# A two-layer decoder trunk: the seven-product form of the first FFN product begins at column tile 2 instead of 4

## The chip, the cores and the metric

The kernel runs on one core of one Trainium2 chip. The metric is the device time of one execution in microseconds, as the median of several executions.

## The reference

Two consecutive layers work on 512 tokens of width 1024 in float32. Each layer is a mixer and then a SwiGLU feed-forward network (FFN). The change is in the FFN, which runs once in each layer:

```
h = modulate(rms_norm(x, ffn_norm[layer]), sh2, sc2)      # (512, 1024)
gate, up = split(h @ w1, 2)                               # w1 (1024, 2 * 2816)
x = x + g2 * ((silu(gate) * up) @ w2)                     # w2 (2816, 1024)
```

## The kernel before

**Precision.** Every large product is made of three matmuls on pairs of fp32r tiles: a value is split into a high part (a copy on ScalarE, line 119) and a low part (a subtraction on VectorE, line 120), and high times high, low times high and high times low are added up in PSUM.

**The first FFN product.** The 2816 columns of gate and of up are cut into NF = 22 column tiles of 128; a tile means the gate columns and the up columns of that number. Both h and the products stand transposed, with tokens along the free dimension. Before the change there are three stretches:

- Tiles 0 and 1 (`ffn_first`, called from `tail`). Four weight tiles, gate 0, up 0, gate 1 and up 1, each in 24 matmuls of 256 columns over tokens 0 to 255 and then, once the second half of h is there, each in 24 more over tokens 256 to 511. The four splits of weights take all four buffers of the weight pools (`whl`), so that the next split can start only when the last matmul of gate 0 is done. `glu` (lines 1279 to 1283) then makes silu(gate) times up of the two tiles.
- Tiles 2 to NP - 1 = 3. `w1_tile` loads 256 gate columns and 256 up columns, `f1` makes each of the four products in 24 matmuls of 512 columns, `glu` ends a tile. Beside it `t_sums` makes the sums of blocks of h that the third stretch needs. It is a generator of four parts: two with four VectorE subtractions in place on `hf` and the split of T2 each (lines 1340 to 1344), then the splits of T3, then those of T1. One part is drawn after each of the four products. `prep` 0 to 2 are also made there.
- Tiles 4 to 21, as NQ = 9 groups of two tiles. A group is one Strassen-like product in seven steps: `prep(s)` makes the weights of step s (VectorE sums of weight blocks and the split), `step_mm(s)` runs 24 matmuls of 256 columns, `post(s)` combines the results. Steps 0 and 1 use plain blocks of h, step 2 uses T2, step 3 T3, step 4 T1, step 5 T4 (split by `t4_split`), step 6 a plain block again. `prep` runs three steps ahead of the matmuls. `q_load(n)` loads the n-th block of 256 columns (gate for even n, up for odd n): into the two buffers `raw`, except that every third one (n % 3 == 2) goes into the two buffers `ada`.

**The second FFN product** follows directly. Its first weights are loaded by `kt_load(0)`, issued in `prep(NS - 7)` into a `raw` buffer, and split in `prep(NS)`; its matmuls show as `w` on lines 123 to 125.

**Order.** TensorE always follows the order of the program. In the block `with tc.manual_schedule(engines=MANUAL)` ScalarE, VectorE and GpSimd follow it too. What stands outside, `glu` of tiles 0 and 1 and the work of `tail`, is placed into the queues of ScalarE and VectorE by the framework's scheduler, and so are the loads on SyncE's queue. [...]

Of the kernel before, what the change touches and what calls it, by code (L numbers as in the profile page):

```python
# [13 lines left out]
AF = mybir.ActivationFunctionType  # L14
ALU = mybir.AluOpType
PSUM = bass.MemoryType.PSUM

P = 128
T = 512
# [3 lines left out]
FF = 2816  # L23
# [46 lines left out]
def trunk(ctx, tc, x, c, positions, ada_w, ada_b, ffn_w1, ffn_w2, ab_w_in, gla_gate_up,  # L70
          dsa_q_norm, dsa_k_norm, ab_w_out, cd_w_in, pool_w, cd_w_out, prm, w0, kc, out):
    nc = tc.nc
    act = nc.scalar.activation
    V = nc.vector
# [18 lines left out]
    def nm(s):  # L93
        uid[0] += 1
        return f"{s}_{uid[0]}"
# [4 lines left out]
    def bank(name="b"):  # L100
        return pp.tile([P, 512], F32, tag="b", name=nm(name))
# [7 lines left out]
    def raw_tile():  # L109
        return rawp.tile([P, 2048], F32, tag="raw", name=nm("raw"))  # L110

    def whl(w=1024):
        return (wp.tile([P, w], F32R, tag="whi", name=nm("whi")),
                wp.tile([P, w], F32R, tag="wlo", name=nm("wlo")))
# [3 lines left out]
    def split(hi, lo, src):  # L118
        act(hi, src, AF.Copy)  # L119
        lo_eng[0].tensor_tensor(lo, src, hi, op=ALU.subtract)  # L120

    def mm3(ps, ah, al, bh, bl, first, last):
        mm(ps, ah, bh, start=first, stop=False)  # L123
        mm(ps, ah, bl, start=False, stop=False)  # L124
        mm(ps, al, bh, start=False, stop=last)  # L125
# [306 lines left out]
    def hT(h, k, a, b):  # L432
        return h.hi[k // 2][:, k % 2, a:b], h.lo[k // 2][:, k % 2, a:b]


    def load_cols(w, c0, n):
        rt = raw_tile()
        r3 = rt[:, 0:8 * n].rearrange("p (k n) -> p k n", k=8)
        nc.sync.dma_start(r3, w.rearrange("(k p) n -> p k n", p=P)[:, :, c0:c0 + n])
        return r3  # L440

    def cols_tile(r3, j):
        hi, lo = whl()
        h3 = hi.rearrange("p (k n) -> p k n", k=8)
        l3 = lo.rearrange("p (k n) -> p k n", k=8)
        split(h3, l3, r3[:, :, j * P:(j + 1) * P])
        return h3, l3
# [7 lines left out]
    def f1(ps, w3, h, a, b, M=P, late=False):  # L455
        if late:
            mm3_late(ps, [(w3[0][:, k, 0:M], w3[1][:, k, 0:M]) + hT(h, k, a, b) + (True,) for k in range(KD)])
            return
        for k in range(KD):
            hh, hl = hT(h, k, a, b)  # L460
            mm3(ps, w3[0][:, k, 0:M], w3[1][:, k, 0:M], hh, hl, k == 0, k == KD - 1)
# [734 lines left out]
    for n in range(2):  # L1196
        ps = bank("gb")
# [12 lines left out]
    op = outproj_first(ab_w_out[0], 0, mixA, g)  # L1210
# [55 lines left out]

        return nxt

    NP = 4
    NQ = (NF - NP) // 2  # L1270

    def ffn(l, h, g, side2=(), last=False, nxt=None):
# [3 lines left out]
        w1, w2 = ffn_w1[l], ffn_w2[l]  # L1276
        gt = {}

        def glu(i, pg, pu):
            s = slot(name="silu")  # L1280
            act(s, pg, AF.Silu)
            gt[i] = slot(name="g")
            V.tensor_tensor(gt[i], s, pu, op=ALU.mult)

        for i in range(2):
            glu(i, h.first[2 * i], h.first[2 * i + 1])

        acc = [[None, None] for _ in range(NTB)]
        gs = [None] * NF
# [9 lines left out]
        def kt(i):  # L1299
            hi, lo = whl()  # L1300
            split(hi, lo, kt.r3[:, i % 2, :])
            if i % 2 and i + 1 < NF:
                kt_load(i + 1)
            if i < NP:
                t = gsplit(gt[i])
# [7 lines left out]
        def mmk(i, q, tb, n):  # L1313
# [4 lines left out]
            t = slice(o + (tb % 2) * P, o + (tb % 2 + 1) * P)  # L1318
            s = slice(n * 512, (n + 1) * 512)
            mm3(acc[tb][n], ghi[:, t], glo[:, t], hi[:, s], lo[:, s], i == 0, i == NF - 1)  # L1320

        def w1_tile(i):
            if i % 2 == 0:
                w1_tile.r = [load_cols(w1, i * P, 256), load_cols(w1, FF + i * P, 256)]
            return [cols_tile(r3, i % 2) for r3 in w1_tile.r]

# [37 lines left out]
        def q_load(n):  # L1366

            c0 = (FF if n % 2 else 0) + (NP + n // 2 * 2) * P
            if n % 3 == 2:
                ts = [ada_tile().rearrange("p (k n) -> p k n", k=4) for _ in range(2)]  # L1370
                for r, t in enumerate(ts):
                    nc.sync.dma_start(t, w1[512 * r:512 * r + 512, c0:c0 + 256].rearrange("(k p) n -> p k n", p=P))
            else:
                r3 = load_cols(w1, c0, 256)
                ts = [r3[:, 0:4], r3[:, 4:8]]
            raw[n] = ts
# [4 lines left out]
        def prep(s):  # L1381
            if s == NS:
                kts.append(kt(0))
            if s == NS + 1:
                kts.append(kt(1))
            if s >= NS:
                return
            q, st = divmod(s, 7)
            (a11, a12), (a21, a22) = raw[2 * q], raw[2 * q + 1]
            if st == 0:  # L1390
                prep.x = gatep.tile([P, D], F32, tag="g", name=nm("s1")).rearrange("p (k n) -> p k n", k=4)
                V.tensor_tensor(prep.x, a21, a22, op=ALU.add)
            if st == 1:
                prep.y = [slot(name="s2").rearrange("p (k n) -> p k n", k=4) for _ in range(2)]
                for p in range(2):
                    c_ = slice(p * P, (p + 1) * P)
                    V.tensor_tensor(prep.y[p], prep.x[:, :, c_], a11[:, :, c_], op=ALU.subtract)
            if st == 2:
                V.tensor_tensor(a21, a11, a21, op=ALU.subtract)
            if st == 3:  # L1400
                for p in range(2):
                    V.tensor_tensor(prep.y[p], a12[:, :, p * P:(p + 1) * P], prep.y[p], op=ALU.subtract)
            hi, lo = (t.rearrange("p (k n) -> p k n", k=4) for t in whl())
            if st in (2, 6):
                for p in range(2):
                    c_ = slice(p * P, (p + 1) * P)
                    split(hi[:, :, c_], lo[:, :, c_], prep.y[p])
            else:
                split(hi, lo, {0: a11, 1: a12, 3: a21, 4: prep.x, 5: a22}[st])
            wq[s] = hi, lo  # L1410
            if st == 3 and 2 * q + 3 < 2 * NQ:
                q_load(2 * q + 3)
            if st == 5 and 2 * q + 4 < 2 * NQ:
                q_load(2 * q + 4)
            if s == NS - 7:
                kt_load(0)
# [31 lines left out]
        def post(s):  # L1448
            q, st = divmod(s, 7)
            i = NP + 2 * q  # L1450
            a, b, c_ = cur["a"], cur.get("b"), cur.get("c")
            if st == 0:
                keep("p1", a)
                if q:
                    fin_t2(i - 2)
            elif st == 1:
                V.tensor_tensor(ends["p1"], b, ends["p1"], op=ALU.add)
            elif st == 2:
                keep("u2", a)
                act(ends["p1"], ends["p1"], AF.Silu)  # L1460
            elif st == 3:
                keep("p7", c_)
            elif st == 4:
                keep("u4", a)
            elif st == 5:
                V.tensor_tensor(ends["u2"], c_, ends["u2"], op=ALU.add)
                V.tensor_tensor(ends["p7"], ends["u4"], ends["p7"], op=ALU.add)
                ends["f"] = ends["p7"]
            else:
                V.tensor_tensor(ends["p1"], ends["p1"], ends["u2"], op=ALU.mult)  # L1470
                gt[i, 0] = ends["p1"]
                keep("s", a, AF.Silu)
                if s == NS - 1:
                    fin_t2(i)

        kts = []
        with tc.manual_schedule(engines=MANUAL):
            nxt_t = w1_tile(2)
            sums = t_sums()
            for i in range(2, NP):  # L1480
                cur_t = nxt_t
                if i + 1 < NP:
                    nxt_t = w1_tile(i + 1)
                    for n in range(3):
                        q_load(n)
                else:
                    prep(0)
                    prep(1)
                pss = []
                for n, w3 in enumerate(cur_t):  # L1490
                    ps = bank("f1")
                    f1(ps, w3, h, 0, T)
                    pss.append(ps)
                    if i == NP - 1 and n == 0:
                        prep(2)
                    next(sums, None)
                glu(i, *pss)
            for s in range(NS):
                prep(s + 3)
                step_mm(s)  # L1500
                post(s)
                if s == 1:
                    t4_split()
            NT_ = 4
            side2 = iter(side2)
            for i in range(NF - NT_):
                if i + 2 < NF:
                    kts.append(kt(i + 2))
                for tb in range(NTB):
                    if tb % 2 == 0:  # L1510
                        next(side2, None)
                    for n in range(2):
                        mmk(i, kts[i], tb, n)
            for _ in side2:
                pass
# [297 lines left out]
```

## Time and profile before

| | |
|---|---|
| median of 3 runs | 1233.04 us (1231.91 to 1239.1) |
| the profiled execution | 1237.57 us, of which the span of the instructions is 1235.8 us |
| mean granted TensorE clock | 0.987 |
| TensorE busy | 1208.7 us, 98% of the span |
| VectorE busy | 876.4 us, 71% |
| ScalarE busy | 580.7 us, 47% |

The median is the time of the kernel. The rows further down come from the profiled execution, whose time is 4.5 us above the median.

### The profile page before, as it was taken

The page shows a single profiled execution, that of the slowest core. Times are in us where ns is not written, and L with a number is a line of the kernel's source. Part 1 is how long each engine was busy: PE and PEld are TensorE (multiplying, and loading weights), DVE is VectorE, ACT ScalarE, POOL GpSimd, SP SyncE. Part 2 cuts the span into 40 slices and gives each one's busy share as a digit, 9 for nine tenths or more (in the row PEclk, how much of TensorE's full clock was granted, in tenths as well). Part 3 has the DMA queues.
Part 4 walks back from the last instruction along what each step waited for, and adds up shares of the span by engine and source line. Part 5 has one row for each costly group of instructions (what it writes and reads, how often), then busy time and mean ns, then how long its engine had stood idle before and what let it go on. Part 6 is the DMA issues. An engine that isn't in the chain of part 4 may idle for free.

```text
span 1235.8 us, 18933 instructions
## 1 busy us (share of the span) xinstructions
PE 1208.7 (98%) x7440; PEld 1039.1 (84%) x7440; DVE 876.4 (71%) x1450; ACT 580.7 (47%) x1107; POOL 154.7 (13%) x153
## 2 busy tenths in 40 slices
PE   7998999999999999999999999999999999999998
PEld 3776777878889999998887877788889999998886
DVE  4486799666768787879796726765777878778333
ACT  4356346645445555553232763642445555553231
POOL 2133135500100000000000363140100000000000
PEclk8998999999999999999999999998999999999999
DMA  9644554321132333328972356322223332426221
GB/s 307 215 136 155 167 189 142 136 86 46 38 123 86 120 93 113 102 70 275 269 276 100 103 170 214 102 68 69 68 69 105 101 119 88 135 88 221 102 69 68
DMA packets 112661, 160.86 MB, mean 130 GB/s; under 512 B 7078, under 2 KB 77750, under 8 KB 112572
## 3 DMA queue, kind: packets, MB, share of 16 engines
q1 hardware_dynamic: 110544, 158.72, 38.9%
q8 instruction: 58, 0.95, 0.3%
q10 hardware_dynamic: 1964, 0.93, 0.3%
q14 instruction: 31, 0.25, 0.1%
q0 software_dynamic: 64, 0.01, 0.0%
HBM read 157.53 MB, written 2.10 MB: 129 GB/s over the span
## 4 chain that ended last, share of the span: by engine, by line
PE 83%; DVE 6%; DMA 5%; ACT 2%; issue 1%; SPq 1%; POOL 1%; ACTq 0%; DVEq 0%; POOLq 0%
PE f L1438 10%; PE f L1437 10%; PE f L1435 10%; PE f L123 6%; PE f L124 5%; PE f L125 5%; PE w L124 4%; PE w L125 4%; PE w L123 4%; DMA ar<-in_ada_w_dram 2%; PE op L123 2%; PE op L125 2%; PE op L124 2%; PE ad L247 2%; PE f L131 2%; PE f L132 1%
## 5 line engine op out<-in xcount | busy, mean ns | idle before, releaser
L119 ACT ACTIVATE whi<-raw 128x1024 fp32r<-128x1024 f32 x164 | 172.0, 1056 | 216.8 <-PE w L125 82.6
L120 DVE TENSOR_TENSOR wlo<-raw,whi 128x1024 fp32r<-128x1024 f32 x124 | 151.2, 1223 | 99.2 <-ACT whi L119 99.2
L1438 PE MATMUL f<-hhi,wlo 128*128 128x256 f32 x576 | 163.0, 283 | 0.0
L1437 PE MATMUL f<-hlo,whi 128*128 128x256 f32 x576 | 163.0, 283 | 0.0
L1435 PE MATMUL f<-hhi,whi 128*128 128x256 f32 x576 | 163.0, 283 | 0.0
L124 PE MATMUL w<-wlo,ghi 128*128 128x512 f32 x352 | 138.0, 392 | 0.6 <-DVE wlo L120 0.4
L123 PE MATMUL w<-whi,ghi 128*128 128x512 f32 x352 | 138.1, 392 | 0.0
L125 PE MATMUL w<-whi,glo 128*128 128x512 f32 x352 | 137.8, 392 | 0.1
L1435 PE MATMUL f<-thi,whi 128*128 128x256 f32 x432 | 122.3, 283 | 0.0
L1437 PE MATMUL f<-tlo,whi 128*128 128x256 f32 x432 | 122.3, 283 | 0.0
L1438 PE MATMUL f<-thi,wlo 128*128 128x256 f32 x432 | 122.3, 283 | 0.0
L120 POOL TENSOR_TENSOR wlo<-raw,whi 128x1024 fp32r<-128x1024 f32 x40 | 97.6, 2446 | 162.0 <-ACT whi L119 144.8
L1442 ACT ACTIVATE e<-f 128x512 f32<-128x512 f32 x90 | 53.8, 598 | 131.5 <-PE f L1438 131.5
L1435 PEld LDWEIGHTS f<-hhi,whi 128*128 128x128 f32 x576 | 110.6, 192 | 0.1
L1437 PEld LDWEIGHTS f<-hlo,whi 128*128 128x128 f32 x576 | 110.6, 192 | 0.1
L1438 PEld LDWEIGHTS f<-hhi,wlo 128*128 128x128 f32 x576 | 110.6, 192 | 0.0
L120 DVE TENSOR_TENSOR wlo<-s,whi 128x512 fp32r<-128x512 f32 (+1 forms) x90 | 68.5, 795 | 45.0 <-ACT whi L119 45.0
L123 PE MATMUL f<-whi,hhi 128*128 128x512 f32 x240 | 96.7, 403 | 1.8 <-DVE iqr L771 1.8
L124 PE MATMUL f<-wlo,hhi 128*128 128x512 f32 x240 | 94.8, 395 | 0.1
L125 PE MATMUL f<-whi,hlo 128*128 128x512 f32 x240 | 94.3, 393 | 0.0
L1435 PEld LDWEIGHTS f<-thi,whi 128*128 128x128 f32 x432 | 82.9, 192 | 0.0
L1437 PEld LDWEIGHTS f<-tlo,whi 128*128 128x128 f32 x432 | 82.9, 192 | 0.0
(341 smaller groups left out, 2639.5 us busy)
## 6 DMA issues: line engine op xcount, KB each, us to landing
raw<-in_ffn_w_dram SPq DMA_DIRECT2D x54, 1024.0 KB, 5.1
ada<-in_ada_w_dram SPq DMA_DIRECT2D x42, 512.0 KB, 4.5
ar<-in_ada_w_dram SPq DMA_DIRECT2D x68, 256.0 KB, 6.1
raw<-in_ab_w_in_dram SPq DMA_DIRECT2D x12, 1024.0 KB, 5.1
ada<-in_ffn_w_dram SPq DMA_DIRECT2D x24, 512.0 KB, 3.6
ar<-in_ada_w_dram SPq DMA_DIRECT2D x64, 128.0 KB, 3.5
raw<-in_cd_w_in_dram SPq DMA_DIRECT2D x8, 1024.0 KB, 5.1
x<-in_x_dram SPq DMA_DIRECT2D x16, 256.0 KB, 5.4
```

What stands on the lines that cost most here:

```text
L119: act(hi, src, AF.Copy)
L120: lo_eng[0].tensor_tensor(lo, src, hi, op=ALU.subtract)
L123: mm(ps, ah, bh, start=first, stop=False)
L124: mm(ps, ah, bl, start=False, stop=False)
L125: mm(ps, al, bh, start=False, stop=last)
L131: mm(ps, ah, bh, start=i == 0, stop=False)
L132: mm(ps, *((ah, bl) if w_is_a else (al, bh)), start=False, stop=False)
L247: mm(ps[32 * g:32 * g + 32, :], condz[:, j, :], rows[j], start=j < 4, stop=j >= 4)
L1435: mm(ps, hi[:, k, c_], bh, start=start and k == 0 and p == 0, stop=False, skip_group_check=not start or p == 1)
L1437: mm(ps, hi[:, k, c_], bl, start=False, stop=False, skip_group_check=not start or p == 1)
L1438: mm(ps, lo[:, k, c_], bh, start=False, stop=k == 3, skip_group_check=not start or p == 1)
L1442: act(ends[name], src, fn)
```

## The change

Tiles 2 and 3 leave the plain form and become the first of now NQ = 10 groups of the seven-product form. NP falls from 4 to 2 and NS from 63 to 70 steps. `w1_tile` and its stretch disappear. The first part of `t_sums` now stands at the head of the block, then `prep(0)`, the second part, `prep(1)`, `prep(2)` and the third part; the fourth part follows `post(0)`. `t4_split` stays after `post(1)`. The arithmetic of `glu` for tiles 0 and 1 is the same, with its helper written out.

```
-    NP = 4
+    NP = 2
     NQ = (NF - NP) // 2
...
-        for i in range(2):
-            glu(i, h.first[2 * i], h.first[2 * i + 1])
+        for i in range(NP):
+            s = slot(name="silu")
+            act(s, h.first[2 * i], AF.Silu)
+            gt[i] = slot(name="g")
+            V.tensor_tensor(gt[i], s, h.first[2 * i + 1], op=ALU.mult)
...
         with tc.manual_schedule(engines=MANUAL):
-            nxt_t = w1_tile(2)
             sums = t_sums()
-            for i in range(2, NP):
-                cur_t = nxt_t
-                if i + 1 < NP:
-                    nxt_t = w1_tile(i + 1)
-                    for n in range(3):
-                        q_load(n)
-                else:
-                    prep(0)
-                    prep(1)
-                pss = []
-                for n, w3 in enumerate(cur_t):
-                    ps = bank("f1")
-                    f1(ps, w3, h, 0, T)
-                    pss.append(ps)
-                    if i == NP - 1 and n == 0:
-                        prep(2)
-                    next(sums, None)
-                glu(i, *pss)
+            for n in range(3):
+                q_load(n)
+            next(sums)
+            prep(0)
+            next(sums)
+            prep(1)
+            prep(2)
+            next(sums)
             for s in range(NS):
                 prep(s + 3)
                 step_mm(s)
                 post(s)
+                if s == 0:
+                    next(sums)
                 if s == 1:
                     t4_split()
```

## Rows read from the trace of the kernel before

**Rows 1.** The page of the profile, parts 1 and 4.
```profile
PE 1208.7 (98%) x7440; PEld 1039.1 (84%) x7440; DVE 876.4 (71%) x1450; ACT 580.7 (47%) x1107; POOL 154.7 (13%) x153
...
PE 83%; DVE 6%; DMA 5%; ACT 2%; issue 1%; SPq 1%; POOL 1%; ACTq 0%; DVEq 0%; POOLq 0%
```

**Rows 2.** Windows: busy time of each engine, granted clock, DMA.
```profile
356.00:377.90 21.90, 21.90 (x99) 18.14 (x98) 18.70 (x25) 8.62 (x14) 0.00 (x0) 1.00 0.29 97
559.00:690.00 131.00, 130.23 (x580) 106.38 (x579) 106.11 (x156) 44.39 (x67) 1.87 (x6) 0.99 0.66 214
894.60:906.10 11.50, 11.50 (x98) 11.50 (x97) 4.69 (x5) 5.45 (x6) 0.00 (x0) 1.00 0.04 13
906.10:928.05 21.95, 21.95 (x100) 18.19 (x99) 18.70 (x25) 8.67 (x14) 0.00 (x0) 1.00 0.29 96
928.05:948.20 20.15, 20.15 (x171) 20.15 (x170) 16.20 (x20) 10.97 (x16) 0.00 (x0) 1.00 0.33 106
```

**Rows 3.** Timeline of TensorE, layer 1: start, length, line, operation.
```profile
906.11 0.40 PE L123 MATMUL f<-hhi,whi 128*128 128x512 f32 x1
...
927.90 0.28 PE L1435 MATMUL f<-hhi,whi 128*128 128x256 f32 x1
...
1109.33 0.40 PE L123 MATMUL w<-whi,ghi 128*128 128x512 f32 x1
```

**Rows 4.** Timeline of VectorE, layer 1, before and beside tiles 2 and 3.
```profile
894.50 0.43 DVE L430 TENSOR_TENSOR hlo<-hf,hhi 128x256 fp32r<-128x256 f32 x1
898.69 1.22 DVE L120 TENSOR_TENSOR wlo<-raw,whi 128x1024 fp32r<-128x1024 f32 x1 [3.77 <-ACT whi L119]
...
906.38 0.69 DVE L1283 TENSOR_TENSOR g<-silu,f 128x512 f32<-128x512 f32 x1 [0.75 <-PE f L125]
...
908.43 0.68 DVE L1340 TENSOR_TENSOR hf<-hf,hf 128x512 f32<-128x512 f32 x1
...
911.93 0.69 DVE L1340 TENSOR_TENSOR hf<-hf,hf 128x512 f32<-128x512 f32 x1
...
917.89 1.22 DVE L1392 TENSOR_TENSOR s<-raw 128x1024 f32<-128x1024 f32 x1
...
920.16 1.29 DVE L1397 TENSOR_TENSOR s<-s,raw 128x512 f32<-128x512 f32 x2
...
922.50 1.22 DVE L1399 TENSOR_TENSOR raw<-raw,raw 128x1024 f32<-128x1024 f32 x1
...
924.84 2.49 DVE L120 TENSOR_TENSOR tlo<-hf,thi 128x512 fp32r<-128x512 f32 x4
...
928.77 1.29 DVE L1402 TENSOR_TENSOR s<-raw,s 128x512 f32<-128x512 f32 x2
929.98 1.22 DVE L120 TENSOR_TENSOR wlo<-raw,whi 128x1024 fp32r<-128x1024 f32 x1
```

**Rows 5.** Timeline of ScalarE, layer 1.
```profile
897.60 1.06 ACT L119 ACTIVATE whi<-raw 128x1024 fp32r<-128x1024 f32 x1 [4.21 <-PE f L124]
...
899.97 0.60 ACT L1281 ACTIVATE silu<-f 128x512 f32<-128x512 f32 x1
```

**Rows 6.** Timeline of SyncE's queue, layer 1.
```profile
887.34 0.37 SPq L439 DMA_DIRECT2D raw<-in_ffn_w_dram  x1
...
888.47 0.37 SPq L439 DMA_DIRECT2D raw<-in_ffn_w_dram  x1
```

**Rows 7.** DMA view, 870 to 960 us: issues, KB, us to landing.
```profile
raw<-in_ffn_w_dram SPq DMA_DIRECT2D x7, 1024.0 KB, 5.1
```

**Rows 8.** Timeline of VectorE, last group of layer 1.
```profile
1090.64 1.29 DVE L1402 TENSOR_TENSOR s<-raw,s 128x512 f32<-128x512 f32 x2
```

**Rows 9.** Timeline of ScalarE, last group of layer 1.
```profile
1101.38 1.05 ACT L119 ACTIVATE whi<-raw 128x1024 fp32r<-128x1024 f32 x1
```

**Rows 10.** Windows around a wait of TensorE in the input projections.
```profile
94.00:100.00 6.00, 1.57 (x19) 0.75 (x19) 5.82 (x10) 5.93 (x12) 0.00 (x0) 0.85 0.18 45
100.00:104.00 4.00, 4.00 (x9) 2.95 (x10) 3.74 (x6) 3.56 (x9) 0.00 (x0) 0.50 0.56 195
```

More of the change, by code (lines that the diff above doesn't have):

```diff
@@ L1277, in ffn @@
         gt = {}
-        def glu(i, pg, pu):
+        for i in range(NP):
             s = slot(name="silu")
-            act(s, pg, AF.Silu)
+            act(s, h.first[2 * i], AF.Silu)
             gt[i] = slot(name="g")
-            V.tensor_tensor(gt[i], s, pu, op=ALU.mult)
-        for i in range(2):
-            glu(i, h.first[2 * i], h.first[2 * i + 1])
+            V.tensor_tensor(gt[i], s, h.first[2 * i + 1], op=ALU.mult)
         acc = [[None, None] for _ in range(NTB)]
@@ L1320, in mmk @@
             mm3(acc[tb][n], ghi[:, t], glo[:, t], hi[:, s], lo[:, s], i == 0, i == NF - 1)
[L1322 to L1325, printed above, removed]
         ht = {}
```

## The prediction

> **What bounds the kernel now.** I read the page first, then the stretch that the change touches, then the queues that feed it. TensorE is busy for 98% of the span and holds 83% of the chain that ended last [rows 1]. The windows say it for the place itself: beside tiles 2 and 3 TensorE is busy for 21.95 of 21.95 us, in the first group of the seven-product form for 20.15 of 20.15, at a granted clock of 1.00, and layer 0 shows the same 21.90 of 21.90 [rows 2]. So nothing there waits for data, and what the stretch costs is what its matmuls cost. VectorE is the engine to watch: it works 18.70 of the 21.95 us beside tiles 2 and 3 and 16.20 of 20.15 in a group, but only 4.69 of 11.50 us in the stretch just before, while TensorE does the second halves of tiles 0 and 1 [rows 2].
>
> **The matmuls.** Removed in each layer: tiles 2 and 3 in the plain form, 4 products of 24 matmuls with 512 columns. They run from 906.11 to 927.90 [rows 3], that is 21.79 us for 96, or 227 ns each. Added: one group of 7 x 24 = 168 matmuls with 256 columns. The nine groups run from 927.90 to 1109.33 [rows 3], 181.43 us, so a group takes 20.16 us, a step 2.88 and a matmul 120 ns. The difference is 21.79 - 20.16 = 1.63 us in each layer, 3.26 in all. Half as many columns cost more than half the time, which is why one eighth fewer columns bring only 7%.
>
> [...]
>
> **The start of the first group.** What hid the sums of h before was the 21.79 us of tiles 2 and 3. Now their only cover is the second halves of tiles 0 and 1 and the first steps themselves. I add up VectorE's queue in layer 1 by rows of the same operations. The sums need only `hf`; VectorE ends its last piece of h at 894.50 + 0.43 = 894.93 and then idles 3.77 us for a split that waits for a weight buffer [rows 4]. Prices [rows 4]: part 1 of the sums takes 911.93 - 908.43 = 3.50, and so does part 2; `prep(0)` 920.16 - 917.89 = 2.27; `prep(1)` and `prep(2)` 2.34 each (922.50 - 920.16 and 924.84 - 922.50); the lows of T3, T1 and T4 half of 2.49 each, 1.25; `prep(3)` 1.21 + 1.22 = 2.43; `prep(4)` and `prep(5)` 1.22 each; the two products of `glu` and the sum in `post(1)` 0.69 each. TensorE wants step s at 906.11 + 2.88 s. In the order of the queue:
>
> - part 1 ends at 898.43, `prep(0)` at 900.70, wanted at 906.11;
> - part 2 at 904.20, a `glu` product at 904.89, `prep(1)` at 907.23, wanted at 908.99;
> - the other `glu` product at 907.92, `prep(2)` at 910.26, wanted at 911.87;
> - T3 at 911.51, `prep(3)` at 913.94, wanted at 914.75;
> - T1 at 915.19, `prep(4)` at 916.41, wanted at 917.63;
> - the sum of `post(1)` at 917.10, T4 at 918.35, `prep(5)` at 919.57, wanted at 920.51.
>
> So VectorE never rests for 25 us and yet is never late; the smallest margin is 0.8 us, at step 3, and step 5 has 0.9. After that a group leaves VectorE 4 us free [rows 2], so the margins grow. If VectorE comes L us later than this, TensorE loses about L - 0.8 in each layer.
>
> **What else must be there.** ScalarE's split for `prep(0)` can start when gate 0's last matmul frees the weight buffer, which the trace shows at 897.60 [rows 5]; 1.06 us later it is done, before VectorE wants it at 899.57. The next three buffers come every 2.88 us after that (24 matmuls of 120 ns), always before VectorE arrives. The loads of blocks 0 and 1 take the place of those of tiles 2 and 3 on SyncE's queue, issued at 887.34 and 888.47 [rows 6]; with 5.1 us to landing [rows 7] they are there near 893.6, and `prep(0)` first reads them at 898.43. I cost both at nothing; if this cover failed, each microsecond past 5.4 at step 0 would be lost.
>
> The silu of `glu` waits for gate 0 and sat behind that first split [rows 5]. Its product is not needed before the second FFN product, so only its place in VectorE's queue matters, which is the second rival below.
>
> The far end changes too. The last group now loads blocks 18 and 19, both into `raw`, so `kt_load(0)` can be issued only after the last `prep` of step 3 has read gate block 18. That read is the pair at 1090.64, ending at 1091.93 [rows 8]; plus 5.1 us to landing is 1097.0, and the first split of w2 starts at 1101.38 [rows 9], a cover of 4.3 us. Nothing lost. The count of weight bytes, sums, splits of h and results is as before.
>
> **The rivals.**
>
> First: VectorE starts late. If the sums take the place of the first split, at 898.69 [rows 4], L is 3.76, TensorE loses 2.96 a layer against the 1.63 gained, and the kernel goes to 1233.04 + 2 x 1.33 = 1235.7. The point from which the change loses is L = 2.4 us. For it: the margin is thin and 25 us of queue have no slack. Against: that split waited for a buffer, the sums wait for none.
>
> Second, the slower side: the products of `glu`, which stand ahead of the block in the program, stay ahead of the sums in VectorE's queue. The second one needs up 1 and started at 906.38 [rows 4]; part 1 then starts at 907.07, `prep(0)` ends at 912.84 (TensorE 6.73 late), `prep(1)` at 918.68 when step 0 ended at 915.72 (2.96 more), `prep(3)` 0.26 more: 9.95 a layer, minus 1.63, twice, is 16.6 us. [...] Against it: before the change the block's own split of tile 2 (898.69) went ahead of both products, so the queue is filled by what is ready [rows 4, 5].
>
> Third: the gain is swallowed in layer 0 by the second FFN product, where the loads are dense (DMA share 0.66). If that stretch is paced by its loads, layer 0 gives nothing and the time is 1231.4. TensorE is busy there for 130.23 of 131.00 us [rows 2], which speaks against it.
>
> **How the numbers follow.** Forecast: TensorE's saving of 3.26 us, nothing lost. In the profiled execution 1237.57 would become 1234.3; taken off the median, 1233.04 - 3.26 = 1229.8. Chances: the forecast with its neighbours 0.81, the first rival 0.08, the second 0.04, the third 0.05, a gain of over 1% from something I don't see 0.02. The range goes up past the first rival's 1235.7 by about 1, since the runs before alone spread over 7 us, and down to 1226, where a saving half again as large meets a low median: 1226 to 1237. One per cent, 12.3 us, is about what a measurement can tell from no change here; only the second rival passes it, and with it a little that I can't name: slower 0.05, faster 0.02, the same 0.93.
>
> **What would show it right or wrong.** In the profile after, line 1435's group should start within 0.3 us of the last matmul of tile 1 (near 356.0 in layer 0), each of ten groups should take 20.16 us, and `w` should start near 1106.1 in layer 1 (1109.33 - 3.26). VectorE's subtractions on `hf` should begin within 0.2 us of the last `hlo`. A gap of TensorE before one of steps 1 to 5, released by `wlo` or `tlo`, means the queue was longer than I added up; one before step 0, released by `wlo`, means the second rival; gaps on lines 123 to 125 in the second product of layer 0 mean the third. The prediction is wrong if the sums don't start by 897.3 (in layer 1, before its shift), or if anything else joins VectorE's queue before step 5.

## The result, and the profile after

The changed kernel takes 1246.15 us (median of 6 runs, 1242.28 to 1251.43) beside 1234.59 us for the kernel before (6 runs): a ratio of 1.0092, 95% interval 1.0067 to 1.0116. By the ratio it is slower by some 11.4 us, 8.3 to 14.3 by the interval, where 3.3 us of gain were forecast. The profiled execution took 1243.88 us with a span of 1242.1.

First the page of the changed kernel: parts 1 and 4, and one group of part 5, followed by the same group in the page of the kernel before.

```profile
PE 1209.0 (97%) x7584; PEld 1045.9 (84%) x7584; DVE 893.4 (72%) x1478; ACT 590.8 (48%) x1125; POOL 154.2 (12%) x153
...
PE 82%; DVE 8%; DMA 4%; ACT 3%; issue 2%; SPq 1%; POOL 1%; ACTq 0%; DVEq 0%; POOLq 0%
...
L1430 PE MATMUL f<-hhi,wlo 128*128 128x256 f32 x640 | 183.9, 287 | 7.7 <-DVE wlo L120 7.7
...
L1438 PE MATMUL f<-hhi,wlo 128*128 128x256 f32 x576 | 163.0, 283 | 0.0
```

Against [rows 1] the engines' shares hardly move; VectorE's part of the last chain goes from 6% to 8%. The last two lines say more: in front of high times low (line 1430 now, 1438 before), TensorE stood idle for 7.7 us in all, for VectorE's low part of the weights, where before it never did. Where that is, the timeline of TensorE in layer 1 shows.

```profile
907.25 0.28 PE L1427 MATMUL f<-hhi,whi 128*128 128x256 f32 x1
907.37 0.28 PE L1429 MATMUL f<-hlo,whi 128*128 128x256 f32 x1
911.13 0.58 PE L1430 MATMUL f<-hhi,wlo 128*128 128x256 f32 x1 [3.48 <-DVE wlo L120]
...
916.98 0.41 PE L1430 MATMUL f<-hhi,wlo 128*128 128x256 f32 x1 [0.35 <-DVE wlo L120]
...
1115.68 0.40 PE L123 MATMUL w<-whi,ghi 128*128 128x512 f32 x1
```

The first group follows tile 1 at once, at 907.25. Its first two matmuls need only the high part of the weights; the third waits 3.48 us for the low part. Step 1 meets another wait of 0.35. I use one measure below, "the stretch": from the first matmul after tile 1 to the first `w` of the second FFN product. Here it is 1115.68 - 907.25 = 208.43 us; before it was 1109.33 - 906.11 = 203.22 [rows 3]; ten groups of 20.16 would be 201.6. So a layer loses 6.83 us against the forecast and 5.21 against before. Layer 0 is the same: 208.42, and 203.23 before. Twice 5.2 is 10.4, which accounts for the ratio within its interval. (The spans of the two profiled executions differ by only 6.3 us, since everything outside the stretches took 4.1 us less in this one; those parts vary by 2 to 4 us between the profiles of the kernels below.) All of the loss lies in the first group: in layer 1, from 934.23 to the first `w` TensorE is busy for 181.44 of 181.44 us, nine groups of 20.16, at a clock of 1.00.

Who was late? VectorE's queue in layer 1, the place of [rows 4]:

```profile
892.24 0.68 DVE L1332 TENSOR_TENSOR hf<-hf,hf 128x512 f32<-128x512 f32 x1
...
895.73 0.75 DVE L430 TENSOR_TENSOR hlo<-hf,hhi 128x256 fp32r<-128x256 f32 x2
896.40 0.69 DVE L1333 TENSOR_TENSOR hf<-hf,hf 128x512 f32<-128x512 f32 x1
...
897.85 0.69 DVE L1335 TENSOR_TENSOR hf<-hf,hf 128x512 f32<-128x512 f32 x1
901.76 0.69 DVE L1283 TENSOR_TENSOR g<-silu,f 128x512 f32<-128x512 f32 x1 [3.22 <-PE f L125]
907.52 0.69 DVE L1283 TENSOR_TENSOR g<-silu,f 128x512 f32<-128x512 f32 x1 [5.07 <-PE f L125]
908.13 0.68 DVE L120 TENSOR_TENSOR tlo<-hf,thi 128x512 fp32r<-128x512 f32 x1
908.73 1.22 DVE L1384 TENSOR_TENSOR s<-raw 128x1024 f32<-128x1024 f32 x1
909.86 1.22 DVE L120 TENSOR_TENSOR wlo<-raw,whi 128x1024 fp32r<-128x1024 f32 x1
911.00 0.68 DVE L1332 TENSOR_TENSOR hf<-hf,hf 128x512 f32<-128x512 f32 x1
...
915.71 1.22 DVE L120 TENSOR_TENSOR wlo<-raw,whi 128x1024 fp32r<-128x1024 f32 x1
```

And ScalarE's, the place of [rows 5]:

```profile
898.81 0.60 ACT L1281 ACTIVATE silu<-f 128x512 f32<-128x512 f32 x1 [2.98 <-PE f L125]
904.57 0.60 ACT L1281 ACTIVATE silu<-f 128x512 f32<-128x512 f32 x1 [5.16 <-PE f L125]
905.07 0.62 ACT L119 ACTIVATE thi<-hf 128x512 fp32r<-128x512 f32 x1
905.59 1.05 ACT L119 ACTIVATE whi<-raw 128x1024 fp32r<-128x1024 f32 x1
```

Read both from the top. The sums start as early as they can: one subtraction even slips in between the last pieces of `hlo`, the other three of part 1 follow at once. Then VectorE's next entry is a product of `glu`, which waits 3.22 us for up 0, and the next the other product, which waits 5.07 us for up 1, the last matmul of tile 1. Only behind it stand the low half of T2 and all of `prep(0)`, though the sum of `prep(0)` needs nothing but loaded weights. On ScalarE both silus stand ahead of T2's high half and of the first split of weights; that split starts at 905.59, where before it started at 897.60 [rows 5]. VectorE thus idled 8.29 us of the time in which the forecast had it make `prep(0)` and part 2. Before the change that split of weights went ahead of the silus and products; now everything of the block but part 1's subtractions goes behind.

Both sums of the prediction, the forecast's and the second rival's, take a queue's entries one after another, and the rows show the two engines at that. On VectorE `tlo` starts at 908.13, 0.61 us after the product ahead of it, although its input `thi` was done at 905.69 and VectorE had stood idle until 907.52. On ScalarE `thi` starts at 905.07, 0.50 us after the silu ahead of it, although the subtractions it reads from were done by 898.54 and ScalarE had stood idle for 5.16 us until 904.57.

Last, the windows of the changed kernel over the wait, the end of the slow steps, and what follows; columns as in [rows 2].

```profile
907.25:911.13 3.88, 0.40 (x4) 0.20 (x2) 3.61 (x5) 0.00 (x0) 0.00 (x0) 0.89 0.00 0
911.13:917.00 5.87, 5.51 (x25) 5.22 (x25) 5.74 (x9) 3.36 (x6) 0.00 (x0) 0.50 0.00 0
917.00:928.00 11.00, 11.00 (x91) 10.95 (x91) 11.00 (x15) 8.72 (x15) 0.00 (x0) 1.00 0.30 98
```

After the wait the granted clock falls to 0.50 for some 6 us. Whether this cost anything on top of the late weights is a question of its own, since VectorE is busy for 5.74 of those 5.87 us.

### The profile page after: what moved, and what is told of

Read it like the earlier page. It is cut to its first block, busy times and chain, and to the rows that moved or that the text cites. A ratio compares the mean times of both kernels' runs of the same rounds, so it can differ in the third digit from the quotient of the medians.

```text
span 1242.1 us, 19272 instructions
## 1 busy us (share of the span) xinstructions
PE 1209.0 (97%) x7584; PEld 1045.9 (84%) x7584; DVE 893.4 (72%) x1478; ACT 590.8 (48%) x1125; POOL 154.2 (12%) x153
## 4 chain that ended last, share of the span: by engine, by line
PE 82%; DVE 8%; DMA 4%; ACT 3%; issue 2%; SPq 1%; POOL 1%; ACTq 0%; DVEq 0%; POOLq 0%
PE f L1430 11%; PE f L1427 11%; PE f L1429 11%; PE f L123 4%; PE w L124 4%; PE w L125 4%; PE w L123 4%; PE f L124 4%; PE f L125 4%; PE op L124 2%; PE op L125 2%; PE op L123 2%; PE ad L247 2%; PE f L131 2%; DMA raw<-in_ffn_w_dram 1%
## 5 line engine op out<-in xcount | busy, mean ns | idle before, releaser
L1430 PE MATMUL f<-hhi,wlo 128*128 128x256 f32 x640 | 183.9, 287 | 7.7 <-DVE wlo L120 7.7
L1427 PE MATMUL f<-hhi,whi 128*128 128x256 f32 x640 | 183.2, 286 | 0.0
L1429 PE MATMUL f<-hlo,whi 128*128 128x256 f32 x640 | 183.2, 286 | 0.0
L1427 PE MATMUL f<-thi,whi 128*128 128x256 f32 x480 | 135.9, 283 | 0.0
L1430 PE MATMUL f<-thi,wlo 128*128 128x256 f32 x480 | 135.8, 283 | 0.0
L1429 PE MATMUL f<-tlo,whi 128*128 128x256 f32 x480 | 135.8, 283 | 0.0
L1430 PEld LDWEIGHTS f<-hhi,wlo 128*128 128x128 f32 x640 | 125.1, 195 | 8.7 <-DVE wlo L120 8.7
L1427 PEld LDWEIGHTS f<-hhi,whi 128*128 128x128 f32 x640 | 125.2, 196 | 0.0
L1429 PEld LDWEIGHTS f<-hlo,whi 128*128 128x128 f32 x640 | 125.1, 195 | 0.0
L1427 PEld LDWEIGHTS f<-thi,whi 128*128 128x128 f32 x480 | 92.1, 192 | 0.0
```

The lines of the kernel that those rows point to most:

```text
L1427: mm(ps, hi[:, k, c_], bh, start=start and k == 0 and p == 0, stop=False, skip_group_check=not start or p == 1)
L1429: mm(ps, hi[:, k, c_], bl, start=False, stop=False, skip_group_check=not start or p == 1)
L1430: mm(ps, lo[:, k, c_], bh, start=False, stop=k == 3, skip_group_check=not start or p == 1)
```

## The experiments

Three theories stood after the result. **A:** the place of `glu` in the queues of ScalarE and VectorE is the whole loss. **B:** VectorE has too much work ahead of the first steps, and the order matters less. **C:** the fallen clock is a good part of the loss. A fourth question was why the order had come out as it did. The ratios below are against the kernel before, run on the same chip; stretches are given as layer 0, layer 1, in us.

**1 and 2. `glu` put into the hand-ordered block, late or in the middle.** Both take silu and product of tiles 0 and 1 out of the place ahead of the block and keep the rest of the change.

```
-        for i in range(NP):
-            s = slot(name="silu")
-            act(s, h.first[2 * i], AF.Silu)
+        sl = {}
+
+        def silu(i):
+            sl[i] = slot(name="silu")
+            act(sl[i], h.first[2 * i], AF.Silu)
+
+        def prod(i):
             gt[i] = slot(name="g")
-            V.tensor_tensor(gt[i], s, h.first[2 * i + 1], op=ALU.mult)
+            V.tensor_tensor(gt[i], sl[i], h.first[2 * i + 1], op=ALU.mult)
```

`glu_late` then calls them after the first group:

```
                 post(s)
                 if s == 0:
                     next(sums)
+                if s == 6:
+                    for i in range(NP):
+                        silu(i)
+                        prod(i)
```

`glu_mid` calls them where the prediction's list had the products:

```
             next(sums)
             prep(0)
+            silu(0)
             next(sums)
+            prod(0)
             prep(1)
+            silu(1)
+            prod(1)
             prep(2)
```

> The change with one edit: silu and product of tiles 0 and 1 stand inside the block, after post(6). Theory A (the place of glu): in the changed kernel VectorE's queue held both glu products, and ScalarE's queue both silus, ahead of the split of T2 and of prep(0), so that TensorE waited 3.5 us before step 0; the rest of the predicted sum holds. Then this kernel has no wait of TensorE in steps 0 to 6, a group takes 20.16 us, and the time is 3.3 us below before, ratio 0.997. Theory B (VectorE's queue is simply too long beside tiles 0 and 1 wherever glu stands): TensorE still waits 2 us or more a layer before steps 1 to 5 and the ratio stays at 1.000 or above.

> silu and product stand inside the block where the prediction had them: silu 0 after prep(0), product 0 after part 2 of the sums, silu 1 and product 1 after prep(1). Theory A: every step's weights are there with at least 0.8 us to spare, no wait, ratio 0.997 like glu_late within 1 us. Theory B: the two products add 1.4 us to the queue ahead of prep(2), so it is slower than glu_late by 1 to 3 us.

Measured: `glu_late` 0.998 (0.9968 to 0.9993), 1232.12 us; `glu_mid` 0.9966 (0.9951 to 0.998), 1230.91 us, the lowest median of all. Both are shown faster than before; that one of them is faster than the other is not shown. The stretches are 201.60, 201.60 in each: exactly ten groups of 20.16, and a gain of 1.62 a layer on 203.22. TensorE of `glu_mid`, from the first step to the second product, without a wait between:

```profile
903.43 0.28 PE L1431 MATMUL f<-hhi,whi 128*128 128x256 f32 x1
...
1105.03 0.40 PE L123 MATMUL w<-whi,ghi 128*128 128x512 f32 x1
```

VectorE of `glu_mid`: the four `wlo` and the two `g` that the prediction's list is about.

```profile
896.50 1.22 DVE L120 TENSOR_TENSOR wlo<-raw,whi 128x1024 fp32r<-128x1024 f32 x1
...
901.14 0.68 DVE L1287 TENSOR_TENSOR g<-silu,f 128x512 f32<-128x512 f32 x1
...
902.94 1.22 DVE L120 TENSOR_TENSOR wlo<-raw,whi 128x1024 fp32r<-128x1024 f32 x1
904.08 0.68 DVE L1287 TENSOR_TENSOR g<-silu,f 128x512 f32<-128x512 f32 x1
...
905.81 1.29 DVE L120 TENSOR_TENSOR wlo<-s,whi 128x512 fp32r<-128x512 f32 x2
...
909.42 1.22 DVE L120 TENSOR_TENSOR wlo<-raw,whi 128x1024 fp32r<-128x1024 f32 x1
```

Here `prep(1)` ends at 904.16 for a step that starts at 903.43 + 2.88 = 906.31, `prep(2)` at 907.10 for 909.19, `prep(3)` at 910.64 for 912.07: margins of 2.15, 2.09 and 1.43, with the two products in the queue. That is theory A. Theory B falls: the same work in another order is never late.

**3. Only the products moved, the silus left outside.** With the helpers of runs 1 and 2:

```
+        for i in range(NP):
+            silu(i)
...
+                if s == 6:
+                    for i in range(NP):
+                        prod(i)
```

> Only the two products are moved, after post(6); the silus stay where the changed kernel has them, ahead of the block. Theory A, by the queue: silu 1 can start only when up 0 and gate 1 are done, 2.6 us before the end of tile 1, so the split of T2 and prep(0) come 1.3 us late for step 0 and prep(1) 3.0 us late for step 1; 4.3 us a layer lost, 1.6 gained, 5.3 us slower than before, ratio 1.004. If the products alone were the cause it would be 0.997, if the silus alone 1.009.

Measured: 1.0074 (1.0052 to 1.0095), 1244.91 us; stretches 207.37, 206.03, that is 5.77 and 4.43 over 201.6. TensorE's waits for its weights in layer 0 (total, count, longest):

```profile
PEld f L1437 <- DVE wlo L120: 3.1, 2, 1.8
PEld f L1434 <- ACT whi L119: 1.0, 1, 1.0
```

And VectorE in layer 0, at the low half of T2:

```profile
355.65 0.69 DVE L120 TENSOR_TENSOR tlo<-hf,thi 128x512 fp32r<-128x512 f32 x1 [7.18 <-ACT thi L119]
```

Layer 1 gave the expected loss, with the clock at 1.00. In layer 0 the clock fell after the waits, to a mean of 0.76 over 363 to 370 us, and it took another 1.3 us, which the expectation did not have; the ratio is above the expected 1.004. So ScalarE's queue alone holds some 4.4 of the 6.8 us: a split of weights behind a silu that waits for tile 1 makes VectorE late even when VectorE's own queue is clear.

**4. The changed kernel, its wait filled with idle matmuls.** This tells theory C: TensorE works through the wait, meant to hold the clock at 1.00, and nothing else changes.

```
             next(sums)
+            wm2 = bank("wm2")
+            for _ in range(16):
+                mm(wm2, idle[:, 0:P], idle, start=True, stop=True)
             for s in range(NS):
```

> The changed kernel with 16 unused matmuls of 512 bf16 columns on the idle tile ahead of step 0, which fill TensorE's wait and keep its clock up; everything else is as in the change. Theory C (the fallen clock is half of the loss: steps 0 and part of 1 ran at a granted clock of 0.50): 2.5 to 3 us less a layer, ratio 1.004. Theory A: prep(1) comes out of VectorE's queue 5.8 us after prep(0) whatever the clock, so step 0 ends sooner and TensorE then waits about 3 us before step 1; the ratio stays at 1.009.

Measured: 1.011 (1.009 to 1.013), 1247.68 us; stretches 209.75, 208.41. Its windows in layer 1, from the fill (910.57 to 913.84) to step 2:

```profile
910.57:914.20 3.63, 3.58 (x19) 1.84 (x18) 3.37 (x4) 0.00 (x0) 0.00 (x0) 1.00 0.00 0
914.20:917.00 2.80, 2.78 (x23) 2.58 (x23) 2.70 (x5) 0.46 (x1) 0.00 (x0) 1.00 0.02 6
917.00:921.00 4.00, 1.56 (x11) 1.15 (x11) 3.97 (x6) 3.39 (x6) 0.00 (x0) 1.00 0.00 0
921.00:935.00 14.00, 14.00 (x118) 13.92 (x117) 14.00 (x20) 10.54 (x16) 0.00 (x0) 1.00 0.41 130
```

The clock is 1.00 throughout, and the stretch is 208.41 against 208.43 with the clock at 0.50. TensorE is through with step 0 at full clock by 917.4 and then stands still before and within step 1, busy for 1.56 of 4.00 us, while VectorE works 3.97 of them. So in the changed kernel the fallen clock cost nothing: VectorE's queue set the pace until step 1, and the slow matmuls ran in time that would have been a wait. Theory C falls. In layer 0 the clock fell later in spite of the fill (0.66 over 366 to 370 us, with TensorE busy for 4.00 of the 4.00), and that layer took 1.3 us more.

**5. The whole of `glu` at the head of the block.** This is the order by which the second rival's sum was made: silu and product of both tiles first, then all of the sums and `prep`.

```
+            for i in range(NP):
+                silu(i)
+                prod(i)
             next(sums)
             prep(0)
```

> The changed kernel with silu and product of both tiles at the head of the block, so that all four subtractions of part 1 stand behind the products, as the prediction's second rival had it. By the sum of that rival TensorE waits 6.7 us before step 0, 3.0 before step 1 and 0.3 later, 9.95 a layer, minus 1.63: 16.6 us slower than before, ratio 1.0135 without anything for the clock, 1.017 with 2 us a layer for it.

Measured: 1.0144 (1.0118 to 1.017), 1253.7 us; stretches 211.32, 211.32 (counted here from 0.12 us after the start of tile 1's last matmul, since the first matmul of step 0 itself waits), a loss of 9.72 a layer. TensorE's waits in layer 0:

```profile
PEld f L1431 <- ACT whi L119: 4.8, 1, 4.8
PEld f L1434 <- DVE wlo L120: 3.2, 2, 1.6
```

The rival's sum without a clock term was 9.95. This order is 2.9 us a layer worse than that of the changed kernel, which is what part 1's four subtractions take (911.00 to 913.89 for the second four, in the changed kernel): there they had run ahead of the products.

**6. VectorE late by a set time.** `glu_late` with ten unused additions of 128x512 on VectorE at the head of the block. They leave the order right and only make the queue longer, as the first rival has it.

```
+            pad = slot(name="pad")
+            for _ in range(10):
+                V.tensor_tensor(pad, f[0, 1], f[1, 1], op=ALU.add)
             next(sums)
             prep(0)
```

> glu_late with ten unused additions of 128x512 (0.60 to 0.69 us each, 6.0 to 6.9 in all) on VectorE ahead of the sums. In glu_late the weights of steps 0 to 3 are there 5.7, 2.75, 3.3 and 2.6 us early. Theory A, by L minus margin: TensorE waits 0.3 to 1.2 us before step 0 and 3.3 to 4.2 in all by step 1 to 3, minus the 1.63 gained, 3.5 to 5 us slower than before, ratio 1.0035, and up to 2 us a layer more if the clock falls. If VectorE's queue is not what step 0 to 3 wait for, 0.997 as glu_late.

Measured: 1.0067 (1.0043 to 1.009), 1244.16 us; stretches 208.67, 206.09: losses of 7.07 and 4.49. Its windows over the first group's start, in both layers:

```profile
355.73:377.00 21.27, 17.69 (x121) 17.08 (x120) 20.61 (x28) 14.29 (x21) 0.00 (x0) 0.84 0.22 70
909.49:930.80 21.31, 17.73 (x143) 17.06 (x142) 21.17 (x29) 15.61 (x23) 0.00 (x0) 1.00 0.24 74
```

With the clock at 1.00 (layer 1) the loss is 4.49 where 3.3 to 4.2 were expected. The ten additions took longer than the expectation had them: the low part for step 0 starts 0.26 us after the step (909.75), where in `glu_late` it starts 6.93 us ahead of it, which is 7.2 us later. Less the smallest margin of `glu_late`, 2.6, that is 4.6, so the rule "VectorE late by L costs L less a margin" holds to a tenth. In layer 0 TensorE had the same waits (one of 1.0 and two that sum to 3.2 us, in either layer), yet the clock fell to a mean of 0.84 and took 2.6 us more. Here the clock costs, unlike in the changed kernel.

**7. What brought the order about, from the side of the kernel before.** Two runs change the kernel before. `sums_first` only draws the first part of the sums ahead of `w1_tile(2)`; `before_glu_in` is the control, with `glu` of tiles 0 and 1 inside the block after tile 2's matmuls and the sums where they were.

```
-            nxt_t = w1_tile(2)
             sums = t_sums()
+            next(sums)
+            nxt_t = w1_tile(2)
```
```
-        for i in range(2):
-            glu(i, h.first[2 * i], h.first[2 * i + 1])
...
+                if i == 2:
+                    for j in range(2):
+                        glu(j, h.first[2 * j], h.first[2 * j + 1])
                 glu(i, *pss)
```

> The kernel before with one part of the change alone: the first part of the sums stands at the head of the block, ahead of the split of tile 2; tiles 2 and 3 stay in the plain form (NP = 4). Theory A: with the sums at its head the block's queues are again filled with both silus and both glu products first, then the split of T2, then the split of gate 2, whose low half comes about 2.7 us after the last matmul of tile 1; the third matmul of tile 2 waits for it, some 2.2 us a layer, so 4 to 5 us slower than before, ratio 1.0035. If the sums at the head cost nothing by themselves and only the seven-product group is hurt, 1.000.

> Control: the kernel before (NP = 4) with glu of tiles 0 and 1 inside the block, beside tile 2. If the gain of glu_late and glu_mid came from moving glu and not from the seven-product group, this is faster than before too, ratio 0.997; theory A has no wait to remove there and expects 1.000.

Measured: `before_glu_in` 1.0002 (0.9985 to 1.002), 1236.33 us, stretches 203.22, 203.22: the place of `glu` was worth nothing before the change. `sums_first` 1.0041 (1.0021 to 1.0062), 1240.89 us, stretches 207.26, 207.25. Moving one part of the sums, with all four tiles still in the plain form, costs 4 us a layer in the profiled execution. Its ScalarE in layer 1:

```profile
903.13 0.60 ACT L1281 ACTIVATE silu<-f 128x512 f32<-128x512 f32 x1 [2.98 <-PE f L125]
908.89 0.60 ACT L1281 ACTIVATE silu<-f 128x512 f32<-128x512 f32 x1 [5.16 <-PE f L125]
909.38 0.62 ACT L119 ACTIVATE thi<-hf 128x512 fp32r<-128x512 f32 x1
909.90 3.88 ACT L119 ACTIVATE whi<-raw 128x1024 fp32r<-128x1024 f32 x4
```

Again both silus come first, then T2, then the splits of weights: the order of the changed kernel, out of the kernel before, by where the sums begin. TensorE then waits 2.6 us for tile 2's low weights. The rest of the 4 us goes with a fallen clock (0.92 over 906.1 to 928.0). That profiled execution, 1247.04 us, was the longest of its twelve runs; the ratio comes to 2.5 us a layer, and how the other executions lost it isn't shown.

**8. `prep(0)` ahead of the sums, `glu` still outside.** If the head of the block decides, a split of weights at the head should go ahead of the silus again.

```
             for n in range(3):
                 q_load(n)
-            next(sums)
             prep(0)
             next(sums)
+            next(sums)
             prep(1)
```

> The changed kernel with one edit: prep(0) stands at the head of the block, ahead of the first part of the sums; glu stays outside. In this order the split of prep(0) leads both queues, as the split of tile 2 did before the change, and the silus and products come between it and the split of T2. Theory A: step 0 starts without a wait; the second glu product starts 0.3 us after the last matmul of tile 1 and holds the split of T2, part 2 and prep(1) behind it, so that prep(1) is done 7.3 us after that point, 4.5 us late for step 1, and 0.2 more at step 3. Minus the 1.63 gained that is 3 us a layer, 6 us slower than before, ratio 1.005, up to 2.6 us a layer more where the clock falls. If only the order at the head mattered and not where glu stands, 0.997.

Measured: 1.0069 (1.0047 to 1.0091), 1244.9 us; stretches 208.47, 207.97. ScalarE in layer 0:

```profile
346.05 1.06 ACT L119 ACTIVATE whi<-raw 128x1024 fp32r<-128x1024 f32 x1 [4.78 <-issue]
347.13 1.28 ACT L1281 ACT_TABLE_LOAD   x1
348.42 0.60 ACT L1281 ACTIVATE silu<-f 128x512 f32<-128x512 f32 x1
351.88 0.60 ACT L1281 ACTIVATE silu<-f 128x512 f32<-128x512 f32 x1 [2.86 <-PE f L125]
352.37 0.62 ACT L119 ACTIVATE thi<-hf 128x512 fp32r<-128x512 f32 x1
```

It does: the split of `prep(0)` is first, then come both silus, and T2 and the split of `prep(1)` stand behind them. TensorE is in time for step 0 and late for step 1 (waits of 2.5 us for the high and 1.8 for the low part, 4.3 together where 4.7 were expected). Then the clock fell, to a mean of 0.84 over 354.4 to 376 us in layer 0 and of 0.86 over 904 to 928 in layer 1; in layer 0 the matmuls came every 0.21 us from 362.39 on, where they came every 0.12 before the waits. The losses are 6.87 and 6.37 a layer. So an edit that wins back step 0 alone moves the wait by one step; only `glu` inside the block removes it. In the four kernels that leave `glu` outside and differ in the head of the block or in NP (before, after, `sums_first`, `prep_first`), the block's first entry on ScalarE went ahead of the silus when it was a split of weights and behind them when it was T2's high half. Why the scheduler ranks the two so, no run here settles.

## Why the prediction was wrong

**The step that failed** is the sentence under the second rival, "before the change the block's own split of tile 2 went ahead of both products, so the queue is filled by what is ready". From it the places of `glu` in the list followed: one product after part 2, the other after `prep(1)`. The built queue had both products right behind part 1's subtractions, and both silus ahead of the first split. One case before the change, a split of weights at the head, was taken for a rule; with a part of the sums at the head the order turned (run 7). The trace of before could only bound the order, not give it, and the rival deserved far more than a chance of 0.04.

With it fell a cover that the prediction costs at nothing, ScalarE's split for `prep(0)`, and the sentence that of the silu "only its place in VectorE's queue matters". The prediction asks when the weight buffer is free, not what stands ahead of the split in ScalarE's queue. The split stood behind both silus and began at 905.59, where the first split began at 897.60 before, in a layer that itself runs 1.14 us later; with the silus alone left outside the loss was 4.43 us a layer (run 3). Two of the prediction's own tests would not have told it: the sums began well before 897.3, and nothing joined VectorE's queue. Only the order was another.

**The second rival** is what happened, and the sign by which it was to be known (a gap of TensorE before step 0, released by `wlo`) is in the timeline, ahead of step 0's third matmul. Its size was 9.95 us a layer; measured 6.83 against ten clean groups. The difference has a cause. Part 1's four subtractions ran ahead of the products, which takes 2.9 off the first term, 6.73, and leaves 3.83; the timeline has the third matmul of step 0 at 911.13, where it would have come at 907.49, 3.64 late. The second term, 2.96 at step 1, comes out: from 911.13 to 916.98, the same matmul of step 1, is 5.85 us for a step of 2.88, 2.97 more. Together 6.6 of the 6.83. With all sums behind the products (run 5) the loss was 9.72. For a fallen clock the expectations of runs 5 and 6 allow up to 2 us a layer, an estimate from the 4 us at 0.50 in [rows 10]; no run shows that figure: the changed kernel lost nothing by its clock (run 4), and layer 0 of `late_pad` lost 2.6 us (run 6).

**The matmuls** were right: 20.16 us a group, 1.62 a layer gained wherever the queue was right (runs 1, 2), with 1.63 forecast. The saving half again as large, with which the prediction's range reaches down to 1226, no run shows: where the first group had no wait, the stretch gave 1.62.

**VectorE's list** was right as a sum of work and wrong as an order. In `glu_mid`, which has the order that the list assumed, the margins at steps 1 to 3 are 2.15, 2.09 and 1.43 where 1.76, 1.61 and 0.81 were worked out, some half a microsecond better; the first subtraction, at 888.42, had slipped in between the pieces of `hlo`.

**The first rival**, VectorE late by L, is the mechanism by which the wrong order costs, but not the cause here; `late_pad` gives its price while the clock stays up.

**The third rival**, layer 0's gain swallowed in the second product, left its sign in one of the two good kernels. In the profile of `glu_mid`, layer 0, TensorE waits there for low parts of weights, 2.0 us in two pieces. VectorE's queue and then TensorE's:

```profile
651.41 3.10 DVE L350 SCALAR_TENSOR_TENSOR acc<-ar,cond,acc 128x512 f32<-128x512 f32 x4
...
656.33 2.35 DVE L120 TENSOR_TENSOR wlo<-raw,whi 128x1024 fp32r<-128x1024 f32 x2
```
```profile
657.61 0.50 PE L124 MATMUL w<-wlo,ghi 128*128 128x512 f32 x1 [1.82 <-DVE wlo L120]
```

The high part was there at 652.52; VectorE came to the low part at 656.33, behind other sums (line 350 and after) that it worked at without a rest. So it was again VectorE's queue that came late, where the rival named the loads; whether late loads of `ar` had delayed those sums is left open. From the first `w` to the first matmul of line 379, which comes behind the second product, it takes 107.97 us in `glu_mid`, 105.26 before and 105.28 in `glu_late`. The profiles of `silu_ahead`, `prep_first`, `glu_first` and `sums_first` have 2.0 to 3.8 us of the same wait, those of before, after and `glu_late` 0.4. `sums_first` keeps tiles 2 and 3 in the plain form, so the wait does not need the change; whether the kernel or the single execution brings it, one profile of each can't tell. It doesn't swallow the gain of `glu_mid` as a rule: 2.5 to 6.1 us by the interval, where this rival left 1.63.

**The far end** was right. In `glu_mid`, the load of the first w2 block on SyncE's queue:

```profile
1087.69 0.37 SPq L452 DMA_DIRECT2D raw<-in_ffn_w_dram  x1
```

and its split on ScalarE:

```profile
1097.09 1.05 ACT L119 ACTIVATE whi<-raw 128x1024 fp32r<-128x1024 f32 x1
```

The split comes 9.4 us after the issue and 8 us ahead of the first `w`, and TensorE starts `w` at 1105.03 without a wait.

## What to carry to other kernels

An edit at the head of a hand-ordered block also decides where work left outside the block lands in the queues of ScalarE and VectorE; a queue sum is only as good as the order it assumes, so take that order from the built program, or put the work into the block. In these queues it was not an instruction's own 0.6 us that counted but what it waited for and what stood behind it: two silus of 0.60 us and two products of 0.69 cost 6.8 us a layer here, against the same change with them placed well. Price both orders, and give them chances by how many cases of the scheduler's choice the trace holds; one is not a rule.

## What the runs showed of the hardware that was not expected

A fallen clock was not a cost by itself: at 0.50 after the wait in the changed kernel, and at 1.00 with the wait filled, layer 1's stretch took 208.43 and 208.41 us, because VectorE set the pace. In `late_pad` the fall did cost: 2.6 us between two layers of one execution.

Nor did the waits alone decide whether it fell. Those two layers have TensorE busy for 17.69 of 21.27 and 17.73 of 21.31 us, with equal waits, and the granted clock was 0.84 in one and 1.00 in the other; `silu_ahead` shows the same (0.76 in layer 0, 1.00 in layer 1). What else decides it, no run here shows. By the two pairs of layers, a forecast would give the clock a term of nought to 2.6 us a layer for such waits, not a fixed price.
